# Four adaLN vectors from VectorE dot products to TensorE column groups, Fourier sums in two PSUM banks

## The chip, the cores and the metric

One core of a Trainium2 chip runs the whole layer as one program. The metric is the device time in microseconds of one execution. Three runs of the kernel before gave a median of 1030.87 us (1029.47 to 1032.01).

## The reference

One encoder layer on x of 1024 positions by 1024 channels, fp32, with a conditioning vector c of 1024:

```
cond = silu(c)
mod = cond @ w_ada + b_ada                      # 6144 values
sh1, sc1, gt1, sh2, sc2, gt2 = split(mod, 6)
h = rms_norm(x, g_pre_mix) * (1 + sc1) + sh1
u, v, rg_g, rg_x, ft_x = split(h @ w_in, ...)   # 1792 columns
y_gm = gelu(u) * spatial(layer_norm(gelu(v)))   # 256 channels
y_rg = two RG-LRU scans of conv(rg_x), gated by gelu(rg_g)   # 512
y_ft = Re(DFT2(ft_x)) @ w_f + b_f               # 256
x = x + gt1 * rms_norm(concat(rms_norm each) @ w_out, g_post_mix)
h = rms_norm(x, g_pre_ff) * (1 + sc2) + sh2
x = x + gt2 * rms_norm(square(relu(h @ w_ff1)) @ w_ff2, g_post_ff)
```

sh1 and sc1 are needed at once for the first normalised input. The other four vectors, gt1, sh2, sc2 and gt2, are needed only after the output projection has begun: these are the four late vectors of the change.

## The kernel before

Activations lie with channels on the 128 partitions and positions along the free dimension, as eight tiles of 1024 positions (`big`). Most products are made in three passes of fp32r on a high and a low part of each operand (`mm3`); ScalarE makes the high part of a weight tile and GpSimd or VectorE the low part (`split`, L170 and L171). All matmuls go through `mm` at L143, so the profile shows one line for them and the tiles tell them apart. A product of plain fp32 operands is one call of `mm` and two MATMUL rows in the trace.

The program is written as one long list of stages. First the input is normalised and the six columns of the input projection for the recurrence and the Fourier branch are made, the first half of the positions and then the second (`zk`). Then come the rest of the input projection (`z`, in full columns of two halves), the recurrence (`rg`, four tiles of two directions each, with matmuls `gz`), the Fourier branch (`ft_fold`, `ft_a`, `ft_b`, with matmuls `fa`, `fx` and `fe`), the spatial gating (`v_mm` with `vp`, `smix` with `rw` and `sp`), three group norms (`norm_group`, `norm_rg`, with matmuls `grs`), the output projection (`op`), the residual and second norm (`resid`) and the feed-forward block (`f`), which takes the last 600 us.

Beside that list run tasks, which are Python generators. A clock counts planned matmul time (`mm` adds columns/2400, four times that for fp32), and after each group of products `pump` runs the tasks that are due; each yields the planned time until its next step. `rg_all` is such a task, the norms are others, and so is `ada_all`, which is spawned right after the recurrence has been joined. This gives the order in which instructions are written; the framework then gives each engine its own order and sets the waits.

The adaLN vectors are dot products on VectorE: `ada(blk)` loads 128 rows of the transposed weight, 128 by 1024 (512 KB), and one instruction multiplies it with the condition, which lies spread over all partitions, and sums along the row into one column of `mod` (L454). There are 32 of them in `ada_all`, and 16 more of the first two vectors at the start of the program, which stay. `vec` adds the bias and, where needed, one and the gain. The loads use the tag `r`, four buffers of 512 KB, which the raw weight tiles of the input and output projections use as well; all of them are issued by SP.

PSUM has eight banks, all of one tag. In `ft_b` each of the two Fourier tiles takes four of them, one for each of the sums Ec, Es, Oc and Os: Es and Ec have 257 columns, Os and Oc 256. ScalarE copies Es and Os out (L648, L649), and four VectorE operations (L651 to L654) combine them with Ec and Oc.

Of the kernel before, what the change touches and what calls it, by code (L numbers as in the profile page):

```python
# [7 lines left out]
F32 = mybir.dt.float32  # L8
F32R = mybir.dt.float32r
AF = mybir.ActivationFunctionType  # L10
ALU = mybir.AluOpType
PSUM = bass.MemoryType.PSUM
MUL, ADD, SUB = ALU.mult, ALU.add, ALU.subtract
# [30 lines left out]
_n = 0  # L44
for _name, _w in (("b_ada", 48), ("g_pre_mix", 8), ("g_post_mix", 8), ("g_pre_ff", 8), ("g_post_ff", 8),
                  ("g_mix_out", 8), ("conv_w", 16), ("conv_b", 4), ("b_a", 8), ("b_x", 8), ("lam", 8),
                  ("ft_b", 2), ("ln_g", 2), ("ln_b", 2)):
    PV[_name] = (_n, _w)
    _n += _w
NPV = _n  # L50


@with_exitstack
def trunk(ctx, tc, xT, c, pv, ident, w_ada, w_k, w_in, w_v, gates, k1, k2, k3, gmft, w_out, w_ff1, w_ff2, out):
    nc = tc.nc
    const = ctx.enter_context(tc.tile_pool(name="const", bufs=1))
    pool = ctx.enter_context(tc.tile_pool(name="pool", bufs=21))
# [19 lines left out]
    def ctile(name, n, dt=F32, bufs=1):  # L77
        return const.tile([128, n], dt, name=name, tag=name, bufs=bufs)

    pvt = ctile("pvt", NPV)  # L80
    idt = ctile("idt", 128)
    ones = ctile("ones", 128)
    eps = ctile("eps", 1)
    mod = ctile("mod", 48)
    ab = ctile("ab", 56)
    sp = ctile("sp", 64)

    ctile("pad0", 8)
    HL = const.tile([128, 8, 2, 1024], F32R, name="HL", tag="HL")
    big = const.tile([128, 8, 1024], F32, name="big", tag="big")  # L90
    ctile("pad1", 8)
    a1, b1, a2, b2, g1, g2, bp1 = (ab[:, i * 8:i * 8 + 8] for i in range(7))

    def col(name, i, n=1):
        a = PV[name][0] + i
        return pvt[:, a:a + n]
# [3 lines left out]
    clock = [0.0]  # L100
# [17 lines left out]
    def spawn(gen, delay=0.0):  # L118
        return Task(gen, delay)
# [137 lines left out]
    cond = tt("cond")  # L257
    cps = pa("cb")
    sq0 = {}
    for h, (a, b) in enumerate(HALF):  # L260
        if h == 1:
            for k in (0, 1):
                sq0[k] = th("sq")
                A.activation(out=sq0[k], in_=big[:, k, 0:512], func=AF.Square)
        mm(cps[h], ones[0:1, :], crow[:, a:b], True, True)
        th0 = A.activation(out=cond[:, a:b], in_=cps[h], func=AF.Tanh, scale=0.5)
        V.scalar_tensor_tensor(out=cond[:, a:b], in0=cond[:, a:b], scalar=1.0, in1=cps[h], op0=ADD, op1=MUL)

    ssl, ssa = [None], [None]

# [89 lines left out]
    ps = [pb("zk%d" % i) for i in range(6)]  # L360
# [82 lines left out]
    ps = [pb("zk0"), pb("zk1")]  # L443
# [5 lines left out]
    evac_z(1, ps, 1, V)  # L449


    def ada(blk):
        r = load(w_ada[blk], tag="r")
        V.scalar_tensor_tensor(out=r, in0=r, scalar=0.5, in1=cond, op0=MUL, op1=MUL,  # L454
                               accum_out=mod[:, blk:blk + 1])

    def vec(dst, blk, gname, one):
        V.tensor_tensor(out=dst, in0=mod[:, blk:blk + 8], in1=col("b_ada", blk, 8), op=ADD)
        if one:
            V.tensor_scalar(out=dst, in0=dst, scalar1=1.0, scalar2=None, op0=ADD)  # L460
        if gname:
            V.tensor_tensor(out=dst, in0=dst, in1=col(gname, 0, 8), op=MUL)

    def ada_all():
        for blk in range(16, 48):
            ada(blk)
            yield ADY[0] if blk < ADY[1] else ADY[2]
        vec(g1, 16, "g_post_mix", False)
        vec(b2, 24, None, False)
        vec(a2, 32, "g_pre_ff", True)  # L470
        vec(g2, 40, "g_post_ff", False)


    xr_t, xs_t = {}, {}
# [110 lines left out]
    kt = {}  # L585
# [43 lines left out]

    def ft_b(t, at, ax):  # L630
        cosE = [kt[1][:, i * 257:i * 257 + 257] for i in range(3)]
        sinE = [kt[2][:, i * 257:i * 257 + 257] for i in range(2)]
        cosO = [kt[3][:, i * 256:i * 256 + 256] for i in range(2)]
        sinO = [kt[3][:, 512 + i * 256:768 + i * 256] for i in range(2)]
        ba = [at[:, j * 128:j * 128 + 128] for j in range(8)]
        ps = [pb("fe") for _ in range(4)]
        Ec, Es, Oc, Os = ps[0][:, 0:257], ps[1][:, 0:257], ps[2][:, 0:256], ps[3][:, 0:256]
        for dst, pairs in ((Es, ((ba[4], sinE[0]), (ba[5], sinE[1]))),
                           (Ec, ((ba[0], cosE[0]), (ba[1], cosE[1]), (ax, cosE[2]))),
                           (Os, ((ba[6], sinO[0]), (ba[7], sinO[1]))),  # L640
                           (Oc, ((ba[2], cosO[0]), (ba[3], cosO[1])))):
            for j, (w, x) in enumerate(pairs):
                mm(dst, w, x, j == 0, j == len(pairs) - 1)
            pump()
        y = big[:, 6 + t, :]
        b = col("ft_b", t)
        sn = [th("sn", F32, 257), th("sn", F32, 256)]
        A.copy(sn[0], Es)  # L648
        A.copy(sn[1], Os)  # L649
        Es, Os = sn  # L650
        V.scalar_tensor_tensor(out=y[:, 0:513:2], in0=Ec, scalar=b, in1=Es, op0=ADD, op1=SUB)  # L651
        V.scalar_tensor_tensor(out=y[:, 514:1024:2], in0=Ec[:, 255:0:-1], scalar=b, in1=Es[:, 255:0:-1], op0=ADD, op1=ADD)
        V.scalar_tensor_tensor(out=y[:, 1:512:2], in0=Oc, scalar=b, in1=Os, op0=ADD, op1=SUB)
        V.scalar_tensor_tensor(out=y[:, 513:1024:2], in0=Oc[:, ::-1], scalar=b, in1=Os[:, ::-1], op0=ADD, op1=ADD)  # L654

# [16 lines left out]
    for m in range(2, 6):  # L672
        p = {m: pb("zk")}
        for k in range(8):
            stage_mm(k, 1, p, (m,))
        evac_z(m, p, 1, V if m % 2 else A)
        if m == 2:
            kt[2] = load(k2, 770, "k2", "t")
            gm = load(gmft, 1024, "gm", "t")
        if m == 3:  # L680
            prep_to(1)
            for i, src, n in ((1, k1, 771), (3, k3, 1024)):
                kt[i] = load(src, n, "k%d" % i, "t")
# [23 lines left out]
            z_full(t, int(q[2]))  # L707
    kt.clear()
    join(trg)
    tad = spawn(ada_all(), 0.0)  # L710
    with tc.issue_after(rgl[0]):
        for t in range(2):
            A.activation(out=big[:, t, :], in_=big[:, t, :], func=AF.Gelu_apprx_tanh)
# [651 lines left out]
def _layout(inp):  # L1365
    import numpy as np

    f = lambda n: np.asarray(inp[n])
    cols = lambda v: v.reshape(-1, 128).T
    dt = f("x").dtype  # L1370
    pv = np.concatenate([
        cols(f("b_ada")[0]), cols(f("g_pre_mix")[0]), cols(f("g_post_mix")[0]), cols(f("g_pre_ff")[0]),
        cols(f("g_post_ff")[0]), cols(f("g_mix_out")[0]), cols(f("rg_conv_w")[0].reshape(-1)),
        cols(f("rg_conv_b")[0]), cols(f("rg_b_a")[0].reshape(-1)), cols(f("rg_b_x")[0].reshape(-1)),
        cols(f("rg_lam")[0].reshape(-1)), cols(f("ft_b")[0].reshape(-1)), cols(f("gm_ln_g")[0]),
        cols(f("gm_ln_b")[0])], axis=1)
    w_in = f("w_in")[0]
    wi = w_in.reshape(8, 128, 14, 128).transpose(2, 1, 0, 3).reshape(14, 128, 1024)[:8]
    wv = w_in[:, 256:512].reshape(2, 4, 128, 256).transpose(0, 2, 1, 3).reshape(2, 128, 1024)
    gates = np.zeros((4, 128, 2, 2, 128), dt)  # L1380
# [18 lines left out]
    k1 = np.concatenate([np.cos(tw * (2 * p * t % S)), np.cos(tw * (2 * p * (t + 128) % S)), c2], axis=1)  # L1399
    u = np.arange(64)  # L1400
    ang = 2 * np.pi * (u[:, None] * u[None, :] % 64) / 64
    ch = np.zeros((128, 2, 128))
    for e in range(2):
        ch[e * 64:e * 64 + 64, 0, e * 64:e * 64 + 64] = np.cos(ang) / 256
        ch[e * 64:e * 64 + 64, 1, e * 64:e * 64 + 64] = np.sin(ang) / 256
    k2 = np.concatenate([np.sin(tw * (2 * p * t % S)), np.sin(tw * (2 * p * (t + 128) % S)), ch.reshape(128, 256)], axis=1)
    k3 = np.concatenate([np.cos(tw * (o * t % S)), np.cos(tw * (o * (t + 128) % S)),
                         np.sin(tw * (o * (t + 1) % S)), np.sin(tw * (o * (t + 129) % S))], axis=1)
# [3 lines left out]
        "c": f("c")[0:1],  # L1412
        "pv": pv,
        "ident": np.eye(128, dtype=f32),
        "w_ada": f("w_ada")[0].T.reshape(48, 128, 1024),
        "w_k": w_in[:, 1024:].reshape(8, 128, 768),
        "w_in": wi,
        "w_v": wv,
# [32 lines left out]
```

## Time and profile before

| | before |
|---|---|
| median of 3 runs | 1030.87 us |
| profiled execution, its own time | 1031.33 us |
| its span, first to last instruction | 1029.5 us |
| mean granted TensorE clock | 0.970 |
| TensorE busy | 963.3 us, 94%, 4756 instructions |
| VectorE busy | 766.4 us, 74% |
| ScalarE busy | 501.0 us, 49% |
| GpSimd busy | 123.8 us, 12% |
| L454, the late dot products | 32, 48.5 us in all with what belongs to them |
| data moved | 191.59 MB, mean 186 GB/s |

The times of the rows are those of one profiled execution, counted from its first instruction. A group of instructions is written as line, engine, operation, output <- inputs, shapes and count. Idle time stands in brackets with the instruction that ended it. The granted clock of a stretch (PEclk) is a mean: 1.00 is 2.4 GHz, and 0.5 is 1.2 GHz.

### The profile page before, as it was taken

To read this page: it belongs to the slowest core of one execution; us is meant where nothing else is said; L and a number is where in the kernel's file an instruction comes from. 1 tells how busy PE (TensorE), PEld (TensorE's weight loads), DVE (VectorE), ACT (ScalarE), POOL (GpSimd) and SP (SyncE) were. 2 spreads that over 40 slices of the span, in tenths; PEclk is the share of its full clock that TensorE was granted. 3 is DMA by queue.
4 is the path that set the end of the run, shared out by engine and by line. 5 is a ranking of instruction groups with operands and counts; after the bars stand their busy time and mean duration, and the time that the engine had idled before them with its cause. 6 is when DMAs were issued, how large, how long until landed. Compare 5 with 4: busy or idle time off the path is not lost.

```text
span 1029.5 us, 13104 instructions
## 1 busy us (share of the span) xinstructions
PE 963.3 (94%) x4756; PEld 804.0 (78%) x4756; DVE 766.4 (74%) x1059; ACT 501.0 (49%) x764; POOL 123.8 (12%) x82
## 2 busy tenths in 40 slices
PE   6789975997899999999999999999999999999995
PEld 2568854896677997988888888888888888888995
DVE  6978888778897678897776776757665777688464
ACT  4454876622454355564544544545444455446311
POOL 4400391321140341000000000000000000000000
PEclk7989987998899999999999999999999999999998
DMA  9740200158235323054343343359899979987532
GB/s 343 286 142 21 82 24 18 62 202 288 102 131 177 129 97 113 32 183 185 132 179 138 133 191 126 123 198 331 297 392 341 362 269 335 328 277 258 187 133 93
DMA packets 80003, 191.59 MB, mean 186 GB/s; under 512 B 8769, under 2 KB 13121, under 8 KB 77890
## 3 DMA queue, kind: packets, MB, share of 16 engines
q1 hardware_dynamic: 76482, 186.56, 50.7%
q10 hardware_dynamic: 3456, 4.20, 1.1%
q8 instruction: 37, 0.61, 0.2%
q14 instruction: 28, 0.23, 0.1%
HBM read 144.58 MB, written 46.14 MB: 185 GB/s over the span
## 4 chain that ended last, share of the span: by engine, by line
PE 73%; DVE 14%; DMA 4%; ACT 4%; issue 3%; POOL 1%; SPq 0%; DVEq 0%; POOLq 0%
PE f L143 59%; PE op L143 6%; DMA raw<-in_w_ada_dram 3%; DVE raw L454 2%; PE z L143 2%; PE zk L143 2%; PE grs L143 1%; PE r L143 1%; DVE raw L291 1%; DVE HL L325 1%; DVE xr L481 1%; DVE big L537 1%; DMA big<-in_xT_dram 1%; ACT av L519 1%; DVE ss L279 1%
## 5 line engine op out<-in xcount | busy, mean ns | idle before, releaser
L143 PE MATMUL f<-x,x 128*128 128x512 f32 x768 | 236.2, 389 | 0.0
L143 PEld LDWEIGHTS f<-x,x 128*128 128x128 f32 x768 | 144.1, 188 | 29.8
L143 PE MATMUL f<-HL,wc 128*128 128x512 f32 x672 | 158.1, 390 | 0.0
L937 ACT CAST x<-R 128x1024 fp32r<-128x1024 f32 x96 | 100.3, 1053 | 110.8 <-DVE R L1131 56.0
L143 PE MATMUL f<-x 128*128 128x512 f32 x384 | 149.4, 389 | 0.0
L143 PEld LDWEIGHTS f<-HL,wc 128*128 128x128 f32 x672 | 125.0, 188 | 28.2 <-ACT big L1067 2.3
L948 DVE TENSOR_TENSOR x<-R,x 128x1024 fp32r<-128x1024 f32 x96 | 116.7, 1221 | 32.1 <-ACT x L937 30.7
L143 PE MATMUL f<-hc,wc 128*128 128x512 f32 x504 | 118.8, 389 | 0.0
L143 PEld LDWEIGHTS f<-hc,wc 128*128 128x128 f32 x504 | 94.6, 188 | 19.7
L143 PE MATMUL op<-HL,hi 128*128 128x256 f32 (+1 forms) x384 | 88.4, 324 | 0.0
L143 PEld LDWEIGHTS f<-x 128*128 128x128 f32 x384 | 72.1, 188 | 15.1
L143 PEld LDWEIGHTS op<-HL,hi 128*128 128x128 f32 x384 | 64.3, 190 | 6.5 <-issue 1.4
L1131 DVE TENSOR_TENSOR R<-R,o 128x512 f32<-128x512 f32 x64 | 43.6, 688 | 33.3 <-DMA o<-in_w_ff_dram 23.9
L143 PE MATMUL z<-HL,hi 128*128 128x512 f32 x192 | 63.3, 433 | 0.7 <-ACT ftg L614 0.7
L171 POOL TENSOR_TENSOR lo<-raw,hi 128x1024 fp32r<-128x1024 f32 x16 | 44.3, 2775 | 155.7 <-ACT hi L170 111.0
L143 PE MATMUL op<-HL,lo 128*128 128x256 f32 (+1 forms) x192 | 61.5, 320 | 0.0
L937 ACT CAST wc<-S 128x1024 fp32r<-128x1024 f32 x28 | 29.5, 1053 | 60.0 <-DVE S L1042 56.4
L454 DVE SCALAR_TENSOR_TENSOR raw<-raw,cond 128x1024 f32<-128x1024 f32 x32 | 48.5, 1521 | 13.4 <-DMA raw<-in_w_ada_dram 13.2
L948 DVE TENSOR_TENSOR wc<-S,wc 128x1024 fp32r<-128x1024 f32 x28 | 34.2, 1222 | 21.6 <-PE f L143 20.0
L143 PEld LDWEIGHTS z<-HL,hi 128*128 128x128 f32 x192 | 38.5, 204 | 11.9 <-issue 3.7
L143 PE MATMUL f<-HL,w 128*128 128x256 f32 x384 | 47.6, 285 | 0.0
L143 PEld LDWEIGHTS f<-HL,w 128*128 128x128 f32 x384 | 46.6, 192 | 0.6 <-issue 0.5
(298 smaller groups left out, 1637.8 us busy)
## 6 DMA issues: line engine op xcount, KB each, us to landing
raw<-in_w_ada_dram SPq DMA_DIRECT2D x48, 512.0 KB, 4.9
R<-Y SPq DMA_DIRECT2D x96, 256.0 KB, 4.8
R<-in_w_ff_dram SPq DMA_DIRECT2D x80, 256.0 KB, 5.0
raw<-in_w_ff_dram SPq DMA_DIRECT2D x32, 512.0 KB, 3.3
Y<-big SPq DMA_DIRECT2D x16, 1024.0 KB, 3.9
o<-in_w_ff_dram SPq DMA_DIRECT2D x64, 256.0 KB, 5.1
Y<-big SPq DMA_DIRECT2D x13, 768.0 KB, 3.4
SS<-R SPq DMA_DIRECT2D x32, 256.0 KB, 5.0
```

What stands on the lines that cost most here:

```text
L143: pe[0] = T.matmul(o, w, x, start=start, stop=stop, skip_group_check=more).ins
L171: (eng or V).tensor_tensor(out=lo, in0=src, in1=hi, op=SUB)
L279: ssl[0] = eng.tensor_tensor(out=ss, in0=ss, in1=sq, op=ADD).ins
L291: V.scalar_tensor_tensor(out=r1, in0=r1, scalar=0.5, in1=cond, op0=MUL, op1=MUL, accum_out=mod[:, 8 + k:9 + k])
L325: V.scalar_tensor_tensor(out=HL[:, k, 1, a:b], in0=xk, scalar=b1[:, k:k + 1], in1=HL[:, k, 0, a:b], op0=ADD, op1=SUB)
L454: V.scalar_tensor_tensor(out=r, in0=r, scalar=0.5, in1=cond, op0=MUL, op1=MUL, accum_out=mod[:, blk:blk + 1])
L481: V.scalar_tensor_tensor(out=xr[:, o0:o1], in0=z[:, i0:i1], scalar=col("conv_w", k * 4 + t), in1=xr[:, o0:o1], op0=MUL, op1=ADD)
L519: A.activation(out=av[:, a:b], in_=rr[h], func=AF.Exp, scale=m4[:, i:i + 1], bias=m4[:, i:i + 1])
L537: V.tensor_tensor_scan(ti, av, ti, 0.0, op0=MUL, op1=ADD)
L937: order[0] = A.copy(dst, src).ins
L948: V.tensor_tensor(out=lo, in0=raw, in1=hi, op=SUB)
L1131: V.tensor_tensor(out=w, in0=w, in1=self.o, op=ADD if q == "M5" else SUB)
```

## The change

`ada_all` now works on a weight laid out the other way round: eight chunks of 128 inputs by 1024 outputs for each vector. The condition is a column per chunk (`cc`, made from c, which now also comes in with the packed small vectors), and that column, spread to 32, is the stationary operand. The 1024 outputs of a chunk are taken as four groups of 256 columns; each group goes to its own 32 partitions of one PSUM bank (`ad`) and is summed over the eight chunks. Then ScalarE copies the bank, two small products with picked columns of the identity turn it into a 128 by 8 vector, and VectorE adds bias, one and gain as before. The task is spawned after the fifth of the six late input columns, with one step every 2.0 us of planned time; the clock books a step as one product of 256 columns, not four.

In `ft_b` Es and Ec share one bank, Os and Oc the other. Es loses its first and last column, which are zero, so that both fit into 512 columns; the two outputs that have no Es part come from a small ScalarE operation.

```diff
-ADY = (1.6, 32, 3)
+ADY = 2.0
...
+    cc = col("c", 0, 8)
+    ch = ctile("ch", 8)
+    A.activation(out=ch, in_=cc, func=AF.Tanh, scale=0.5)
+    V.tensor_scalar(out=ch, in0=ch, scalar1=0.5, scalar2=0.5, op0=MUL, op1=ADD)
+    V.tensor_tensor(out=cc, in0=cc, in1=ch, op=MUL)
...
     def ada_all():
-        for blk in range(16, 48):
-            ada(blk)
-            yield ADY[0] if blk < ADY[1] else ADY[2]
-        vec(g1, 16, "g_post_mix", False)
-        vec(b2, 24, None, False)
-        vec(a2, 32, "g_pre_ff", True)
-        vec(g2, 40, "g_post_ff", False)
+        for v, (dst, gname, one) in enumerate(((b2, None, False), (a2, "g_pre_ff", True),
+                                               (g1, "g_post_mix", False), (g2, "g_post_ff", False))):
+            i = (1, 2, 0, 3)[v]
+            p = pb("ad")
+            for k in range(8):
+                r = load(w_adn[i, k], tag="r")
+                for g in range(4):
+                    mm(p[g * 32:g * 32 + 32, 0:256], cc[:, k:k + 1].to_broadcast([128, 32]), r[:, g * 256:g * 256 + 256],
+                       k == 0, k == 7, True)
+                clock[0] -= 3 * 4 * 256 / 2400.0
+                yield ADY
+            sb = th("adr", F32, 256)
+            A.copy(sb, p[:, 0:256])
+            yield 1.0
+            q = p[:, 256:264]
+            for j in range(2):
+                mm(q[:, j:8:2], sb[:, j * 128:j * 128 + 128], idt[:, 0:128:32], True, True)
+            V.tensor_tensor(out=dst, in0=q, in1=col("b_ada", 16 + 8 * i, 8), op=ADD)
...
-        ps = [pb("fe") for _ in range(4)]
-        Ec, Es, Oc, Os = ps[0][:, 0:257], ps[1][:, 0:257], ps[2][:, 0:256], ps[3][:, 0:256]
+        ps = [pb("fe") for _ in range(2)]
+        Es, Ec, Os, Oc = ps[0][:, 0:255], ps[0][:, 255:512], ps[1][:, 0:256], ps[1][:, 256:512]
...
-        V.scalar_tensor_tensor(out=y[:, 0:513:2], in0=Ec, scalar=b, in1=Es, op0=ADD, op1=SUB)
+        A.activation(out=y[:, 0:513:512], in_=Ec[:, 0:257:256], func=AF.Identity, bias=b)
+        V.scalar_tensor_tensor(out=y[:, 2:512:2], in0=Ec[:, 1:256], scalar=b, in1=Es, op0=ADD, op1=SUB)
...
+        if m == 4:
+            tad = spawn(ada_all(), 0.0)
...
     join(trg)
-    tad = spawn(ada_all(), 0.0)
```

## Rows read from the trace of the kernel before

**Rows 1.** The page, first part: busy time, share and instructions of each engine.
```profile
PE 963.3 (94%) x4756; PEld 804.0 (78%) x4756; DVE 766.4 (74%) x1059; ACT 501.0 (49%) x764; POOL 123.8 (12%) x82
```

**Rows 2.** Windows: stretch, its length, each engine's busy time, PEclk, DMA share, GB/s.
```profile
114.00:166.00 52.00, 35.34 (x159) 28.28 (x157) 46.64 (x35) 36.79 (x59) 33.80 (x26) 0.87 0.16 58
166.00:177.40 11.40, 8.87 (x31) 6.97 (x31) 9.04 (x9) 11.15 (x18) 1.69 (x1) 0.80 0.00 1
177.40:247.40 70.00, 70.00 (x400) 61.85 (x398) 53.77 (x66) 28.69 (x39) 22.66 (x9) 0.98 0.45 156
247.40:275.00 27.60, 16.52 (x117) 12.26 (x115) 25.95 (x49) 11.86 (x19) 4.76 (x2) 0.88 0.48 179
275.00:311.00 36.00, 34.16 (x143) 26.87 (x144) 30.86 (x49) 18.48 (x29) 10.86 (x4) 0.91 0.40 139
311.00:1029.00 718.00, 705.22 (x3571) 600.05 (x3569) 505.79 (x702) 334.31 (x502) 24.84 (x25) 1.00 0.57 205
```

**Rows 3.** Waits of TensorE, 100 to 410 us: total, times, longest.
```profile
PE fe L143 <- ACT at L75: 9.6, 1, 9.6
PE grs L143 <- DVE dg L219: 8.2, 2, 6.7
PE grs L143 <- DVE gss L552: 4.4, 1, 4.4
...
PE gz L143 <- DVE big L535: 2.5, 1, 2.5
PE fe L143 <- DVE big L654: 2.1, 1, 2.1
...
PE grs L143 <- DVE gss L805: 0.3, 1, 0.3
```

**Rows 4.** The chain that ended last, around 253 us: start, length, what.
```profile
252.10 1.23 DVE raw L454 x2
...
253.65 0.61 DVE dg L219
```

**Rows 5.** Instructions on the tile `raw`, the late dot products: ns min/median/max, first, last start.
```profile
L454 DVE SCALAR_TENSOR_TENSOR raw<-raw,cond x32: 1183/1224/3410, 199.6 to 323.5; 128x1024 f32<-128x1024 f32 x32
```

**Rows 6.** Timeline of TensorE, 254 to 275 us: start, length, what.
```profile
254.40 2.05 PE L143 MATMUL grs<-dg,ones 128*128 128x512 f32 x2 [6.66 <-DVE dg L219]
...
258.31 0.40 PE L143 MATMUL z<-HL,lo 128*128 128x512 f32 x1
258.63 0.66 PE L143 MATMUL rw<-gm,ones 128*64 128x128 f32 x8
...
260.42 3.50 PE L143 MATMUL sp<-gm,vs 128*64 128x128 f32 x60
263.85 0.73 PE L143 MATMUL z<-HL,hi 128*128 128x512 f32 x2
264.42 0.39 PE L143 MATMUL z<-HL,lo 128*128 128x512 f32 x1
...
269.63 0.61 PE L143 MATMUL z<-HL,hi 128*128 128x512 f32 x2
270.09 0.39 PE L143 MATMUL z<-HL,lo 128*128 128x512 f32 x1
274.89 1.54 PE L143 MATMUL grs<-ones,gss 128*128 128x1 f32 x8 [4.42 <-DVE gss L552]
```

**Rows 7.** Timeline of TensorE, 151 to 170 us, the Fourier matmuls.
```profile
151.70 1.06 PE L143 MATMUL fa<-ftg,fo 128*128 128x128 f32 x8
...
152.82 1.90 PE L143 MATMUL fe<-k,at 128*128 128x257 f32 x8
...
154.99 1.89 PE L143 MATMUL fe<-k,at 128*128 128x256 f32 x8
166.44 3.48 PE L143 MATMUL fe<-k,at 128*128 128x257 f32 x8 [9.56 <-ACT at L75]
```

**Rows 8.** Timeline of VectorE, around 270 us: a late dot product.
```profile
270.27 1.21 DVE L454 SCALAR_TENSOR_TENSOR raw<-raw,cond 128x1024 f32<-128x1024 f32 x1
```

More of the change, by code (lines that the diff above doesn't have):

```diff
@@ L46 @@
                   ("g_mix_out", 8), ("conv_w", 16), ("conv_b", 4), ("b_a", 8), ("b_x", 8), ("lam", 8),
-                  ("ft_b", 2), ("ln_g", 2), ("ln_b", 2)):
+                  ("ft_b", 2), ("ln_g", 2), ("ln_b", 2), ("c", 8)):
     PV[_name] = (_n, _w)
@@ L53, in trunk @@
 @with_exitstack
-def trunk(ctx, tc, xT, c, pv, ident, w_ada, w_k, w_in, w_v, gates, k1, k2, k3, gmft, w_out, w_ff1, w_ff2, out):
+def trunk(ctx, tc, xT, c, pv, ident, w_ada, w_adn, w_k, w_in, w_v, gates, k1, k2, k3, gmft, w_out, w_ff1, w_ff2, out):
     nc = tc.nc
@@ L86, in trunk @@
     sp = ctile("sp", 64)
-    ctile("pad0", 8)
     HL = const.tile([128, 8, 2, 1024], F32R, name="HL", tag="HL")
     big = const.tile([128, 8, 1024], F32, name="big", tag="big")
-    ctile("pad1", 8)
+    ctile("pad", 16)
     a1, b1, a2, b2, g1, g2, bp1 = (ab[:, i * 8:i * 8 + 8] for i in range(7))
@@ L449, in trunk @@
     evac_z(1, ps, 1, V)
[L452 to L462, printed above, removed]
-    def ada_all():
-        for blk in range(16, 48):
-            ada(blk)
-            yield ADY[0] if blk < ADY[1] else ADY[2]
-        vec(g1, 16, "g_post_mix", False)
-        vec(b2, 24, None, False)
-        vec(a2, 32, "g_pre_ff", True)
-        vec(g2, 40, "g_post_ff", False)
+    def ada_all():
+        for v, (dst, gname, one) in enumerate(((b2, None, False), (a2, "g_pre_ff", True),
[16 more added lines that the diff above has]
+            V.tensor_tensor(out=dst, in0=q, in1=col("b_ada", 16 + 8 * i, 8), op=ADD)
+            if one:
+                V.tensor_scalar(out=dst, in0=dst, scalar1=1.0, scalar2=None, op0=ADD)
+            if gname:
+                V.tensor_tensor(out=dst, in0=dst, in1=col(gname, 0, 8), op=MUL)
     xr_t, xs_t = {}, {}
@@ L631, in ft_b @@
         cosE = [kt[1][:, i * 257:i * 257 + 257] for i in range(3)]
-        sinE = [kt[2][:, i * 257:i * 257 + 257] for i in range(2)]
+        sinE = [kt[2][:, i * 257 + 1:i * 257 + 256] for i in range(2)]
         cosO = [kt[3][:, i * 256:i * 256 + 256] for i in range(2)]
@@ L646, in ft_b @@
         b = col("ft_b", t)
-        sn = [th("sn", F32, 257), th("sn", F32, 256)]
+        sn = [th("sn", F32, 255), th("sn", F32, 256)]
         A.copy(sn[0], Es)
@@ L650, in ft_b @@
         Es, Os = sn
-        V.scalar_tensor_tensor(out=y[:, 0:513:2], in0=Ec, scalar=b, in1=Es, op0=ADD, op1=SUB)
-        V.scalar_tensor_tensor(out=y[:, 514:1024:2], in0=Ec[:, 255:0:-1], scalar=b, in1=Es[:, 255:0:-1], op0=ADD, op1=ADD)
+        A.activation(out=y[:, 0:513:512], in_=Ec[:, 0:257:256], func=AF.Identity, bias=b)
+        V.scalar_tensor_tensor(out=y[:, 2:512:2], in0=Ec[:, 1:256], scalar=b, in1=Es, op0=ADD, op1=SUB)
+        V.scalar_tensor_tensor(out=y[:, 514:1024:2], in0=Ec[:, 255:0:-1], scalar=b, in1=Es[:, ::-1], op0=ADD, op1=ADD)
         V.scalar_tensor_tensor(out=y[:, 1:512:2], in0=Oc, scalar=b, in1=Os, op0=ADD, op1=SUB)
@@ L1375, in _layout @@
         cols(f("rg_lam")[0].reshape(-1)), cols(f("ft_b")[0].reshape(-1)), cols(f("gm_ln_g")[0]),
-        cols(f("gm_ln_b")[0])], axis=1)
+        cols(f("gm_ln_b")[0]), cols(f("c")[0])], axis=1)
     w_in = f("w_in")[0]
@@ L1414, in _layout @@
         "ident": np.eye(128, dtype=f32),
-        "w_ada": f("w_ada")[0].T.reshape(48, 128, 1024),
+        "w_ada": f("w_ada")[0][:, 0:2048].T.reshape(16, 128, 1024),
+        "w_adn": f("w_ada")[0][:, 2048:].reshape(8, 128, 4, 1024).transpose(2, 0, 1, 3),
         "w_k": w_in[:, 1024:].reshape(8, 128, 768),
```

## The prediction

> **What bounds the kernel now.** First the page: TensorE is busy 94% of the span, VectorE 74%, ScalarE 49% [rows 1]. A change therefore shows in the time only where TensorE stands still, runs at a lower granted clock, or gets more or less to do. So I next cut the span where the change lies and looked at how much TensorE is missing in each stretch [rows 2]. From 177.4 to 247.4 us it is busy 70.00 of 70.00 us, and after 311 us it is dense again but for 12.8 us in 718, which the change does not touch. The missing time is in three places: 16.7 us in 114 to 166, 2.5 us in 166 to 177.4, and 11.1 + 1.8 us in 247.4 to 311. Third, the waits of TensorE name who ended these holes [rows 3]: before 177 us the recurrence's and the Fourier branch's hand-offs (ScalarE `at` 9.6 us, VectorE L535 2.5, L654 2.1), after 247 us the norm's `dg` (8.2 us, of which one is 6.7) and `gss` (4.4 and 0.3). The longest of the late ones, 6.66 us, is the present price of the adaLN vectors: `dg` comes at 253.65 behind two dot products of L454 that had waited for their weights [rows 4, 6]. The chain of waits runs through those loads and dots for some 58 us before, but beside a full TensorE, where they cost nothing.
>
> **What goes.** 32 dot products of 1.224 us leave VectorE, 39 us in all [rows 5]. Worth on the path: the 6.66 us hole goes, since `dg` needs only a short chain that starts with sums made at 241 us. With it goes the slow restart: from 254.40 to 258.63 TensorE does two `grs` matmuls of 512 columns and six `z`, in 4.23 us; at the pitches seen elsewhere (0.216 per 256 columns of fp32, so 0.43; 0.23 for a `z`) it is 2.24 us, so 2.0 are clock [rows 6, 7]; the granted clock of that stretch is 0.88 [rows 2]. The hole of 4.42 us before 274.89 stays in the main: it starts from matmuls `sp` and runs through VectorE work that remains; one dot of 1.2 us in it, at 270.27, goes [rows 8]. The other `dg` wait (8.2 - 6.7 = 1.5) and the `gss` L805 wait (0.3) have dots ahead of them and go. In 275 to 311 the clock is 0.91, which is 0.09 x 36 = 3.2 us; half of it, 1.6, I count as given back because the hole ahead of it is only shortened. Sum of what comes back: 6.7 + 2.0 + 1.2 + 1.5 + 0.3 + 1.6 = 13.3 us. Bounds: 6.7 (the one hole alone) and 6.7 + 2.0 + 4.4 + 1.5 + 0.3 + 3.2 = 18.1 (every hole and all the clock).
>
> **What TensorE gets.** 32 steps (four vectors x eight chunks) of four fp32 products, 32 columns stationary, 256 moving, each to its own 32 partitions of PSUM. An fp32 product is two MATMUL rows (the two `grs` above are one call), so a step is eight instructions. One with 256 columns takes (1.89 - 0.38)/7 = 0.216 us when they follow one another [rows 7]. No row shows four column groups. The nearest row has two: `sp`, 64-column products alternating between two halves of the array, 60 in 3.50 us, that is (3.50 - 0.27)/59 = 0.055 each, against (1.06 - 0.28)/7 = 0.112 for the same 128 columns on the whole array [rows 6, 7]. Two halves do overlap by a full factor of two. Bounds of a step: 8 x 0.216 / 4 = 0.43 with four abreast, 0.86 if only pairs overlap, 1.73 if none does. I take 0.43: the factor with two was complete. To that comes the change between whole array and groups. Going in, `z` at 258.31 to `rw` at 258.63 is 0.32 instead of 0.23; going out, the last `sp` at 263.65 to `z` at 263.85 is 0.20 instead of 0.11, and `z` to `z` (two, 0.57 instead of 0.46, as at 269.63 to 270.09) loses 0.11 more [rows 6]. Together 0.29 per visit, with a floor of 0 if the next step follows at once. A step: 0.72 us; 32 make 23 us. Each vector ends with four instructions of 4 columns for the turn into columns, about 0.11 each, 0.45. The planner books 0.43 a step, so its clock runs ahead of the engine.
>
> The Trainium skill (TensorE: Matmul & The Clock Gate, Packing small matmuls) reports three column groups giving 2.38 times, less than three. Carried to four it would be some 3.2 times, an estimate from that page: 0.55 for the products of a step instead of 0.43, and 2 us more on the path over 18 steps. The full factor in the two-group row speaks against it, and no row here has more than two.
>
> **Where the steps fall.** The task now starts after the fifth of the six late input columns, about 114 us, not after the recurrence. Steps are due every 2.0 us of planned matmul time and are looked at only between groups of 0.64 or 1.28, so about 2.4. At the planner's own prices (0.213 for 512 columns, four times that in fp32) the matmuls between 114 and 166.4 come to some 29 us, those from 166.4 to 177.4 to 6.5, those from 177.4 to 247.4 to 63. So about 12 steps run before 166.4, two between, and the other 18 after 177.4; the last is planned some 20 us before 247.4.
> - The 12 before 166.4: 8.7 us plus one turn, beside 16.7 us of holes. Cost nothing. If the holes were not there, or if a step came ahead of a matmul that the recurrence waits for, up to 9.2.
> - 166.4 to 177.4: two steps, +1.4. The wait for L654 is for PSUM banks of the first Fourier tile; with two banks per tile instead of four I count its 2.1 us as gone. The first eight Fourier matmuls take 3.48 us after a 9.56 us hole, and 1.90 when TensorE was running [rows 7]; with steps in the hole, 1.6 comes back. Against that, +1.3 for what is put into the hand-offs: the sums of Es now wait in one bank behind six matmuls of Ec (6 x 0.216 = 1.3), one more bank is held by the vector for eight steps, and VectorE and ScalarE wait for the turn. Net -1.0, bounds -3.7 and +6.
> - After 177.4: TensorE is full there, so 18 x 0.72 = 13.0 and three turns 1.3: +14.3. If ready steps are drawn forward into the earlier holes, down to 8.
> The loads (32 of 512 KB) only move earlier, into stretches with a DMA share of 0.16 and 0.00 [rows 2], and share four buffers with the weights to be split. SP's queue is where a late step would hold a weight load behind it; these weights are used 20 us after their load is due, so nothing. The condition as a column (one tanh and two operations on 8 columns at the start) lies beside the input loads: nothing. The small ScalarE operation on two Fourier columns, twice: inside the 1.3.
>
> **Sum.** -1.0 + 14.3 - 13.3 = 0.0 against the profiled execution's own 1031.33 us, which lies 0.46 above the median shown. Forecast 1030.9 us: no change. About 0.3%, 3 us, is what a measurement of this kernel can tell from none.
>
> **Rivals.**
> - Only pairs of column groups overlap (slower). Place: the 20 steps after 166.4. Price: 0.86 - 0.43 = 0.43 each, +8.6: 1039.5. It decides as soon as a step takes more than 0.9 us. For it: no row has four; against: the pair is perfect. With no overlap at all, 20 x 1.3 = +26: 1057.
> - The freed banks let ready work fill the 9.6 us hole (faster). The next input products have their operands before 166 us and stand behind the Fourier sums; if banks, not the order written out, kept them there, 8 us of the 10 come forward: 1023. For it: the L654 wait shows a shortage of banks. Against: the 9.6 us hole ended with `at`, which the change does not hasten.
> - The held bank or the buffers lengthen the recurrence (slower): L535 already keeps `gz` 2.5 us for a bank [rows 3]; with one fewer, the next release of that chain and the turn's wait on VectorE make +5: 1036.
> - The late holes stay although the dots are gone, because the same VectorE work is waited for: only 6.7 of 13.3 comes back, +6.6: 1037.5.
>
> **From this to the numbers.** Forecast 0.40 (own range 1026 to 1036); pairs 0.14, no overlap 0.04; filled hole 0.25; bank 0.10; holes stay 0.07. Range 1020 to 1042: it leaves out no overlap, the far ends of pairs and filled hole, under 0.2. Faster by over 0.3%: 0.24 of the filled hole and 0.12 of the forecast's lower end, 0.36. Slower: all of pairs and no overlap, most of the next two and 0.05 of the forecast, 0.36. Within: 0.28.
>
> **What would show it.** The `ad` matmuls: eight in a step with starts that give 0.43 us, not 0.86 or 1.7, and about 0.3 us lost around them. The wait for `dg` of 6.7 us gone. The stretch from the first full input column to the last `z` before the first `grs` some 14 us longer, the stretch to 311 some 13 us shorter. The `fe` wait for L654 gone, the one for `at` still there. The prediction is wrong if the hole before 166 closes, if a step costs over 0.9 us, or if holes appear in the full stretch.

## The result and the profile after

The changed kernel takes 1059.67 us (median of four runs, 1058.04 to 1061.14) against 1030.61 for the kernel before on the same chip: a ratio of 1.0281, 95% interval 1.026 to 1.0302. The forecast was 1030.9, range 1020 to 1042: wrong by 28.8 us, and outside its range. The profiled execution has a span of 1057.2 us, 27.7 more than before.

First part of the page after, beside [rows 1]:

```profile
PE 995.5 (94%) x5028; PEld 809.5 (77%) x5028; DVE 725.6 (69%) x997; ACT 505.3 (48%) x773; POOL 126.2 (12%) x82
```

VectorE lost 41 us of work, TensorE is busy 32 us more. Where the time came in, from the first starts of tiles (us from the span's start):

| landmark | before | after | later by | this stretch alone | forecast of it |
|---|---|---|---|---|---|
| first full column of `z` | 177.4 | 184.1 | 6.7 | +6.7 | -1.0 |
| last `z` ahead of the norm's first `dg` matmul | 247.4 | 264.7 | 17.3 | +10.6 | +14.3 |
| first `op` | 288.1 | 310.4 | 22.3 | +5.0 | -13.3 |
| first `f` | 389.4 | 414.1 | 24.7 | +2.4 | 0 |
| end | 1029.5 | 1057.2 | 27.7 | +3.0 | 0 |

Windows of the changed kernel with these bounds, columns as in [rows 2]:

```profile
114.00:166.00 52.00, 42.36 (x237) 28.02 (x236) 44.01 (x33) 31.35 (x49) 32.24 (x26) 0.87 0.50 175
166.00:184.10 18.10, 15.93 (x95) 12.52 (x94) 14.69 (x13) 18.04 (x32) 3.28 (x1) 1.00 0.31 117
184.10:264.60 80.50, 80.48 (x527) 61.82 (x526) 29.77 (x55) 31.43 (x47) 22.45 (x8) 1.00 0.42 151
264.60:311.00 46.40, 30.53 (x170) 23.73 (x170) 35.79 (x44) 27.00 (x39) 17.09 (x6) 0.81 0.23 80
```

The dense stretch stayed dense (80.48 of 80.50 us). The stretch that was to get shorter has 15.9 us without TensorE work. Waits of TensorE, 100 to 410 us, beside [rows 3]:

```profile
PE grs L143 <- DVE gss L564: 15.9, 2, 9.3
PE gp L143 <- DVE big L388: 4.8, 1, 4.8
PE ad L143 <- DMA raw<-in_w_adn_dram: 4.8, 3, 2.7
PE fe L143 <- ACT at L75: 1.6, 1, 1.6
```

The waits for `dg` are gone as forecast, and so is all but 1.6 us of the one of 9.6 us for `at`, which was to stay. In their place stand two long waits for `gss` and, early, new ones of `gp` and `ad`.

The price of a step came out as forecast. The tile `ad`, and TensorE's timeline around a step in the dense stretch:

```profile
L143 PE MATMUL ad<-raw,pvt x256: 379/379/636, 114.2 to 238.2; 128*32 128x256 f32 x128
```

```profile
186.90 0.63 PE L143 MATMUL z<-HL,lo 128*128 128x512 f32 x2
187.46 0.64 PE L143 MATMUL ad<-raw,pvt 128*32 128x256 f32 x8
188.02 1.20 PE L143 MATMUL z<-HL,hi 128*128 128x512 f32 x4
189.06 0.63 PE L143 MATMUL z<-HL,lo 128*128 128x512 f32 x2
```

Four steps that stood ready together, in the hole ahead of `at`:

```profile
166.55 1.93 PE L143 MATMUL ad<-raw,pvt 128*32 128x256 f32 x30
```

Thirty instructions of 0.379 us each are done in 1.93, so eight take (1.93 - 0.38)/29 x 8 = 0.43 us: the four groups run fully side by side. Among `z`, from the `z` group at 186.90 to the next at 188.02 is 1.12 us instead of some 0.46, and that next group of four takes 1.04 instead of 0.93. A step costs 0.66 + 0.11 = 0.77 us (forecast 0.72), and the others of the dense stretch cost the same.

The long wait for `gss` is made on VectorE. GpSimd's and VectorE's timelines of the changed kernel:

```profile
250.38 4.76 POOL L171 TENSOR_TENSOR lo<-raw,hi 128x1024 fp32r<-128x1024 f32 x2 [15.27 <-ACT hi L170]
273.13 14.73 POOL L171 TENSOR_TENSOR lo<-raw,hi 128x1024 fp32r<-128x1024 f32 x5 [18.00 <-ACT hi L170]
```

```profile
273.91 1.40 DVE L570 SCALAR_TENSOR_TENSOR big<-big,pvt,grs 128x512 f32<-128x512 f32 x2
275.22 0.74 DVE L786 SCALAR_TENSOR_TENSOR sg<-sp,pvt,tg 128x512 f32<-128x512 f32 x1
275.88 0.93 DVE L820 TENSOR_TENSOR gss<-gss,gsq 128x512 f32<-128x512 f32 x1
276.74 3.43 DVE L808 TENSOR_TENSOR big<-big,sg 128x1024 f32<-128x1024 f32 x1
280.08 2.83 DVE L820 TENSOR_TENSOR gss<-gss,gsq 128x512 f32<-128x512 f32 x1
282.84 2.82 DVE L171 TENSOR_TENSOR HL<-big,HL 128x512 fp32r<-128x512 f32 x1
285.59 2.82 DVE L820 TENSOR_TENSOR gss<-gss,gsq 128x512 f32<-128x512 f32 x1
288.33 0.68 DVE L564 TENSOR_TENSOR gss<-gss,gsq 128x512 f32<-128x512 f32 x1
```

GpSimd makes five low parts of output-projection weights in one block. Beside it, VectorE operations of 128 by 512 with two SBUF operands take 2.8 us (the first of them, at 275.88, only 0.93) instead of the 0.68 that the last row shows just after the block; those with one operand in PSUM (`sg` from `sp`, L570 from `grs`) keep their 0.70 to 0.74. The Trainium skill (SBUF — State Buffer, Who interferes with whom) states that a VectorE instruction with two SBUF inputs contends with a GpSimd instruction that reads SBUF, and that one with at most one SBUF input outside the two-port modes does not. The rows agree in both halves.

In the kernel before the low parts stand apart, but one of them falls beside the VectorE operation for which TensorE waits in the 4.42 us hole of [rows 6]. Two of its GpSimd rows, and that operation:

```profile
271.93 2.36 POOL L171 TENSOR_TENSOR lo<-raw,hi 128x1024 fp32r<-128x1024 f32 x1 [4.40 <-ACT hi L170]
283.74 4.71 POOL L171 TENSOR_TENSOR lo<-raw,hi 128x1024 fp32r<-128x1024 f32 x2 [9.45 <-ACT hi L170]
```

```profile
272.01 2.82 DVE L552 TENSOR_TENSOR gss<-gss,gsq 128x512 f32<-128x512 f32 x1
```

So the price of a low part beside this chain, 2.1 us, stood in the trace that the prediction was made from.

### The profile page after: what moved, and what is told of

Read it like the earlier page. It is cut to its first block, busy times and chain, and to the rows that moved or that the text cites. A ratio compares the mean times of both kernels' runs of the same rounds, so it can differ in the third digit from the quotient of the medians.

```text
span 1057.2 us, 13585 instructions
## 1 busy us (share of the span) xinstructions
PE 995.5 (94%) x5028; PEld 809.5 (77%) x5028; DVE 725.6 (69%) x997; ACT 505.3 (48%) x773; POOL 126.2 (12%) x82
## 4 chain that ended last, share of the span: by engine, by line
PE 83%; DVE 7%; POOL 3%; ACT 2%; issue 2%; DMA 2%; SPq 0%; DVEq 0%; POOLq 0%; ACTq 0%
PE f L143 57%; PE op L143 7%; PE z L143 6%; PE zk L143 5%; PE vp L143 2%; PE ad L143 1%; PE grs L143 1%; PE gz L143 1%; PE r L143 1%; DMA xh<-in_xT_dram 1%; DVE gss L820 1%; DMA big<-in_xT_dram 1%; DVE HL L332 1%; DVE xh L1267 0%; PE rx L143 0%
## 5 line engine op out<-in xcount | busy, mean ns | idle before, releaser
L143 PE MATMUL f<-HL,wc 128*128 128x512 f32 x672 | 161.7, 395 | 0.0
L952 ACT CAST x<-R 128x1024 fp32r<-128x1024 f32 x96 | 100.2, 1053 | 110.5 <-DVE R L1146 56.3
L143 PE MATMUL op<-HL,hi 128*128 128x256 f32 (+1 forms) x384 | 91.2, 332 | 0.0
L143 PE MATMUL zk<-HL,wkb 128*128 128x512 f32 x192 | 48.7, 401 | 0.0
```

What stands on the lines that cost most here:

```text
L952: order[0] = A.copy(dst, src).ins
```

## The experiments

**Which half of the change.** The Fourier sums alone; the vectors alone; the vectors begun where the old task began.

```diff
# e1: before, with ft_b of the change
# e2: changed, with ft_b of before
# e3: changed, and:
-        if m == 4:
-            tad = spawn(ada_all(), 0.0)
     join(trg)
+    tad = spawn(ada_all(), 0.0)
```

> The kernel before with the Fourier part of the change alone (two PSUM banks, the small ScalarE operation). Theory H (hand-offs): the two banks are no cause of the 29 us; 1029 to 1032, the wait of fe for L654 (2.1 us) gone and nothing else moved by more than 2 us. Rival F (the shared banks delay the recurrence): the first full input column starts some 6 us later than 177.4 us, as in the changed kernel (184.1), and the time is about 1037.

> The changed kernel with the Fourier sums back in four banks. Theory H: the late vectors alone make the loss, 1058 to 1064. Rival F: with the four banks back, 6 us or more come back, 1053 or less. A third way: four banks and the held bank together starve PSUM, and it is slower than 1064.

> The changed kernel, but the vectors' task starts where it did before, after the recurrence has been joined. The loads then share the four buffers with the output projection's weights again. Theory W (the loss after 264 us comes from the output projection's weights: their loads no longer alternate with the vectors' loads, so five GpSimd splits run in one block, 273 to 288 us, beside VectorE operations that take 2.8 us instead of 0.7): no such block, the first full input column again near 177 us, all 32 steps on the path (32 x 0.77 + 2 = 27) less the 6.7 us hole: about 1045 to 1052. Rival O (the holes come from the order in which VectorE got its work without the dot products): the holes of 9.3 and 6.5 us stay, 1058 or more.

Each ratio is to the kernel before on the same chip. Measured: e1 1029.54 (ratio 0.9993, 0.9979 to 1.0007), e2 1062.26 (1.0304, 1.0277 to 1.0331), e3 1047.27 (1.0165, 1.0143 to 1.0187). The Fourier half is neutral, as counted, and the wait for L654 is gone. The vectors, with the constants and padding that came with them, make the whole loss. Begun late, they leave the recurrence alone and GpSimd's low parts stand apart; the two long holes are not there, and the loss is 1.65% instead of 2.81%.

**The late stage.** The vectors left out altogether; then the low parts moved; then only the dots left out.

```diff
# e4: before, and (late vectors' sums are zero):
-            ada(blk)
+            if blk == 16:
+                V.memset(mod[:, 16:48], 0.0)
# e5: e4, and; e8: changed, and:
-        wlist.append((("out", k), w_out[k], G))
+        wlist.append((("out", k), w_out[k], V))
# e6: before, with a one-column operation in place of each late dot
```

> The kernel before with the 32 late loads and dot products left out, their sums taken as zero: that part of the result is left out. It shows by itself what their absence gives back. The prediction's term: 13.3 us come back, 1017. Theory W: the 6.7 us hole goes, but the output projection's weights come in one block and open holes of some 10 to 15 us around 270 to 290: 1030 to 1040. Rival O expects the same holes, but with VectorE operations of normal length (0.7 us) in them.

> As e4 (late loads and dot products left out, their sums zero), and the low parts of the eight output projection weights made on VectorE instead of GpSimd. Theory W (GpSimd's block of splits stretches the VectorE operations on the way to the third norm from 0.7 to 2.8 us): no stretched operation, the hole of 9.4 us before 268 shrinks to 5 or less although VectorE gets 8 x 1.2 us more to do, 1026 to 1031. Rival O (order alone): the hole stays at 8 to 10 us, 1034 or more.

> The kernel before with the 32 late loads kept in the four shared buffers, but each dot product replaced by one operation on a single column, so the late vectors are not computed. Theory W: as long as these loads alternate with the output projection's weights, the GpSimd splits stay apart, the holes of 9.4 and 6.5 us of e4 do not come, and VectorE's relief shows: 1018 to 1027, with a hole before dg left where VectorE still waits for a load. Rival O (VectorE's order without the long operations makes the holes): 1033 or more, as e4.

> The changed kernel with the low parts of the eight output projection weights on VectorE instead of GpSimd. Theory W: the hole of 9.3 us before 289 shrinks to 5 or less, 1052 to 1056. Rival O: hole and time stay, 1058 to 1062.

Measured: e4 1034.02 (1.0037, 1.0021 to 1.0052), e5 1021.81 (0.9903, 0.9879 to 0.9927), e6 1038.08 (1.0058, 1.0038 to 1.0078), e8 1047.47 (1.0147, 1.0119 to 1.0175).

e4 refutes the term that failed, by itself: without dots, loads or steps the kernel is not 13.3 us faster than before but 0.37% slower. GpSimd's block and TensorE's waits in e4:

```profile
252.11 14.71 POOL L171 TENSOR_TENSOR lo<-raw,hi 128x1024 fp32r<-128x1024 f32 x5 [17.91 <-ACT hi L170]
```

```profile
PE grs L143 <- DVE gss L553: 16.0, 2, 9.4
```

With the eight low parts on VectorE, which gets more work by that, e4 gets 12.2 us shorter (e5) and the changed kernel 12.2 as well (e8) by the medians, 13.8 by the ratios; both are faster than theory W had them. VectorE's operations of the norm in e5, then TensorE's waits in e5 and in e8:

```profile
258.19 0.68 DVE L806 TENSOR_TENSOR gss<-gss,gsq 128x512 f32<-128x512 f32 x1
258.78 1.22 DVE L794 TENSOR_TENSOR big<-big,sg 128x1024 f32<-128x1024 f32 x1
259.92 0.68 DVE L806 TENSOR_TENSOR gss<-gss,gsq 128x512 f32<-128x512 f32 x1
260.52 0.69 DVE L171 TENSOR_TENSOR HL<-big,HL 128x512 fp32r<-128x512 f32 x1
261.12 0.68 DVE L806 TENSOR_TENSOR gss<-gss,gsq 128x512 f32<-128x512 f32 x1
```

```profile
PE grs L143 <- DVE gss L553: 6.2, 2, 5.7
```

```profile
PE grs L143 <- DVE gss L564: 6.3, 2, 5.8
```

So GpSimd's low parts beside the norm cost 12 us. With them out of the way one sees what the absence of the dots is worth. The stretch from the last `vp` to the first `op`, in the kernel before and in e5, columns as in [rows 2]:

```profile
237.00:288.10 51.10, 40.02 (x220) 31.53 (x218) 41.88 (x80) 22.06 (x34) 11.51 (x5) 0.87 0.48 172
```

```profile
236.60:280.70 44.10, 37.89 (x219) 29.93 (x218) 35.06 (x63) 26.66 (x40) 0.00 (x0) 0.94 0.18 60
```

TensorE stands idle 6.2 us instead of 11.1: the `dg` hole is gone (6.7) and the `gss` hole of 4.4 has shrunk to 0.5, but one of 5.7 has opened ahead of the last `gss` sum before `op`, where the kernel before does not wait:

```profile
287.25 0.95 PE L143 MATMUL grs<-ones,gss 128*128 128x1 f32 x8
```

The same matmuls take 37.9 us instead of 40.0, at a granted clock of 0.94 instead of 0.87. In all e5 gains 7.0 us in this stretch.

What keeps the low parts apart in the kernel before is not the sharing of the buffers with the late loads, as theory W had it: e6 keeps all 32 loads and has a block all the same (and a hole of 7.3 us).

```profile
259.42 11.96 POOL L171 TENSOR_TENSOR lo<-raw,hi 128x1024 fp32r<-128x1024 f32 x4 [22.40 <-ACT hi L170]
```

What is left is the dots' time on VectorE, which holds the norm's operations and the buffers longer. That is argued by elimination and not shown, and through which of the two it works was not separated.

**Other orders and the low parts elsewhere.**

```diff
# e7: e1, and:
+    tgf = [spawn(norm_group((6, 7), 256), 1.0)]
     v_mm(0)
     v_mm(1)
...
-    tgf = [spawn(norm_group((6, 7), 256), 1.0)]
# e9: before, and; e12: e3, and:
-        wlist.append((("out", k), w_out[k], G))
+        wlist.append((("out", k), w_out[k], V))
```

> The kernel before with the Fourier part of the change, and the Fourier group's norm task started ahead of the two v products instead of behind the layer norm; nothing left out. If the 6.7 us hole before dg is only a matter of where this norm stands, it closes and the restart's 2 us with it: 1021 to 1024. Rival: VectorE's wait for a weight load stands ahead of dg there too and holds TensorE inside the v products: 1028 or more.

> The kernel before with one edit: the low parts of the eight output-projection weight tiles are made by VectorE, not GpSimd; the dot products stay on VectorE. Theory W (the GpSimd low parts cost only where several of them follow one another beside the norm's VectorE work): in the kernel before they stand apart, so little is won, and VectorE gets 8 x 1.2 = 10 us more beside 39 us of dots: 1028 to 1032 us. Rival 1 (each GpSimd low part costs wherever it stands): some 12 us come back as with the vectors left out, 1019. Rival 2 (VectorE, with dots and low parts, becomes late for the norm): holes of TensorE before the norm sums grow, 1035 or more.

> The changed kernel with the vectors begun only after the recurrence (as in the earlier run at 1047 us), and the eight output-projection low parts on VectorE. Theory W (GpSimd low parts cost where they form a block beside the norm): there the GpSimd low parts already stood apart, so 1043 to 1048 us. Rival (each of them costs wherever it stands): 12 us come back, 1035.

Measured: e7 1038.64 (1.0061, 1.0038 to 1.0083): the `dg` hole, 5.4 us, only moved ahead into the `vp` matmuls, and two of 5.7 for `gss` came behind it. e9 1034.53 (1.0025, 1.0007 to 1.0042): between theory W and the second rival; the holes for `dg` and `gss` shrink to 5.0 and 2.1, but `op` now waits 4.1 us for low parts from VectorE. e12 1042.92 (1.0116, 1.0091 to 1.0142): 4.4 us better than e3, a little more than W allowed and far from the rival's 12. The low parts cost 12 us as a block; where they stand apart, moving them won 4.4 us (e3 to e12) or nothing (before to e9).

**The early loss.** Without the late loads; with a bank for each step.

```diff
# e10: changed, and:
-                r = load(w_adn[i, k], tag="r")
-                    mm(..., r[:, g * 256:g * 256 + 256],
+                    mm(..., pvt[:, 0:1].to_broadcast([128, 256]),
# e11: changed, and:
-            p = pb("ad")
             for k in range(8):
+                p = pb("ad")
...
-                       k == 0, k == 7, True)
+                       True, True, True)
```

> The changed kernel without the 32 late weight loads: the column-group products take a resident column, repeated, as moving operand (so the four vectors are not the layer's). Products, banks and turns stay. Open is the early loss: first full input column 6.7 us later than before. Theory S (the steps wait for loads that wait for shared buffers, and hold TensorE behind them): the two waits of 1.8 and 2.7 us near 155 and 158 us go and with them what hangs on them; first full column at 179 us or earlier, total about 1053. Theory H (the PSUM bank held through eight steps takes it from the gated products): the 4.8 us wait for a bank near 135 us stays, first full column at 183 to 185, total 1058 to 1061. Theory T (the steps themselves lie on the path there, no hole takes them): also 183 to 185 us, but without the 4.8 us wait.

> The changed kernel with a new PSUM bank for each step, given back after it, and no summing over the eight chunks (so the four vectors hold the last chunk only). Loads, products and turns stay. Theory H (held bank): the 4.8 us wait near 135 us goes, first full input column at 178 to 180 us, total about 1054. Theory S (shared load buffers): the waits near 155 and 158 us stay, first full column at 182 to 185 us, total 1057 to 1061.

TensorE's timeline: the changed kernel, then e11. The matmuls `gp` make `ftg`, which every `fa` reads; `at` is ScalarE's copy of `fa`.

```profile
134.85 2.08 PE L143 MATMUL gp<-gm,k 128*128 128x128 f32 x8 [4.82 <-DVE big L388]
...
155.03 0.64 PE L143 MATMUL ad<-raw,pvt 128*32 128x256 f32 x8 [1.81 <-DMA raw<-in_w_adn_dram]
...
158.35 1.07 PE L143 MATMUL ad<-raw,pvt 128*32 128x256 f32 x4 [2.68 <-DMA raw<-in_w_adn_dram]
...
170.04 2.00 PE L143 MATMUL fe<-k,at 128*128 128x255 f32 x8 [1.56 <-ACT at L75]
```

```profile
135.09 1.08 PE L143 MATMUL ad<-raw,pvt 128*32 128x256 f32 x8 [3.37 <-DVE big L388]
...
166.60 2.07 PE L143 MATMUL fe<-k,at 128*128 128x255 f32 x4 [10.08 <-ACT at L75]
168.60 1.08 PE L143 MATMUL ad<-raw,pvt 128*32 128x256 f32 x8
```

The same place in e10, and a row of ScalarE in the changed kernel:

```profile
168.01 3.78 PE L143 MATMUL fe<-k,at 128*128 128x255 f32 x8 [3.23 <-ACT at L75]
```

```profile
163.83 0.27 ACT L639 COPY ax<-fx 128x128 f32<-128x128 f32 x1 [7.46 <-PE fx L143]
```

Measured: e10 1056.44 (1.0244, 1.0218 to 1.027), first full column at 183.2 us, `at` at 168.0 instead of 170.0, the 4.8 us wait still there. So the loads make 2.0 of the 3.6 us by which `at` is late, but only 1 us of the early loss, and some 2 behind it. ScalarE's row shows how: the steps' waits for loads at 155 and 158 us stand ahead of `fa` and `fx` in TensorE's order, and ScalarE's copy of `fx`, which stands ahead of the recurrence's next operations and of `at` in its own, waits 7.46 us. e11 1061.34 (1.0296, 1.0272 to 1.0321): `gp` no longer waits (a step waits there instead, 3.37 us for the same operation), no step waits for a load at 155 or 158 us, and `at` comes at 166.6 as before [rows 7], not 170.0. So the held bank and the loads together make `at` 3.4 us late; e11 takes both waits away, and the bank's own share was not separated. But e11 gains nothing: six steps now stand between `at` and the first full column, which comes at 186.6. H was right that `at` would come back and wrong on the time.

**The placement.** The last 5.4 us of the table lie where no step runs. The long weight stretch of the feed-forward block, in the kernel before and after:

```profile
L143 PE MATMUL f<-HL,wc x672: 387/389/435, 438.3 to 705.7; 128*128 128x512 f32 x168
```

```profile
L143 PE MATMUL f<-HL,wc x672: 388/394/418, 462.4 to 734.1; 128*128 128x512 f32 x168
```

The same matmuls take 271.7 us instead of 267.4. The mean difference of the start times of neighbours with `HL` as moving operand is 233.3 ns for 512 columns against 227.3, already in the `zk` of the first 114 us, and so in every later stretch. Products on the same weight tiles whose moving operand is a working tile (`f<-hc,wc`) keep 226.7 and 227.7 ns, so it is not the place of the weight tiles alone. The change also moves tiles: in front of the working tiles it adds 8 columns to the packed vectors, 8 for `ch` and 8 of padding, and takes away 8 in front of `HL`. `HL` stays where it was, and the working tiles lie 16 columns, 64 bytes, further from it.

```diff
-    ctile("pad0", 8)
...
-    ctile("pad1", 8)
+    ctile("pad", 16)
# e13: changed, without the line ctile("pad", 16): tiles lie as before
# e14: before, ctile("pad1", 24): 64 bytes higher; e16: ctile("pad1", 16): 32 bytes
# e15: e12, without ctile("pad", 16)
```

> The changed kernel with only the 16 columns of padding ahead of the working tiles taken out; every tile after them lies 64 bytes lower, as in the kernel before. Found in the traces: products of 512 columns with HL follow one another every 233.3 ns in the changed kernel from the first input columns on (40 to 114 us, long before a vector step), 226.7 ns in the kernel before and in every run with its placement. Theory P (the place of the weight tiles against HL sets the pitch): 226.7 ns again, and some 8 to 10 us come back (292 zk, 288 z, 672 in the feed-forward block and about 250 in the output projection, 6.5 ns each): 1050 us. Rival (the pitch hangs on something else in the changed program): 233.3 ns and 1057 to 1061.

> The kernel before with 16 more columns of padding, so that the working tiles lie where the changed kernel has them (64 bytes higher); nothing else. Theory P: 233.3 ns pitch and 8 to 10 us slower, 1039 to 1041. Rival: 226.7 ns and 1029 to 1032.

> The kernel before with 8 more columns of padding: working tiles 32 bytes higher, half of the shift of the change. Theory P says the pitch hangs on the distance to HL but not how: bounds 226.7 ns (1029 to 1032) and 233.3 ns (1039 to 1041); if 32 bytes give a third value, the place counts in steps smaller than 64 bytes. Rival: no change in pitch and time.

> The changed kernel without that padding, with the vectors begun after the recurrence and the output-projection low parts on VectorE (with padding: 1042.9). Theory P: 1033 to 1035, that is the 32 steps cost about what the placement and the GpSimd block did not. Rival: 1041 to 1045.

Measured: e13 1056.69 (1.025, 1.0224 to 1.0276), e14 1036.29 (1.0061, 1.0045 to 1.0078), e16 1036.36 (1.0061, 1.0046 to 1.0076), e15 1038.07 (1.0079, 1.0062 to 1.0095). The stretch in e13 (one line was taken out, so L142) and in e14:

```profile
L142 PE MATMUL f<-HL,wc x672: 387/390/436, 464.6 to 731.9; 128*128 128x512 f32 x168
```

```profile
L143 PE MATMUL f<-HL,wc x672: 388/395/419, 441.0 to 712.6; 128*128 128x512 f32 x168
```

267.3 and 271.6 us: the pitch follows the padding in both directions, and 32 bytes do the same as 64. Theory P holds for the pitch (only the working tiles were moved, never `HL`); its price was put too high (8 to 10). Exchanged both ways it is worth, by the ratios, 6 us in the kernel before and 3 in the changed one, 4 from e12 to e15. Products of 256 columns go the other way, 120 to 117 ns. From the first `op` to the end e13 takes 742.6 us, the changed kernel 746.8 and the kernel before 741.4, so 4.2 of the 5.4 us are the placement; the other 1.2 were not followed.

**The dots moved instead of replaced.**

```diff
# e17: e1, and; e18: e17 with the eight low parts on VectorE:
-            yield ADY[0] if blk < ADY[1] else ADY[2]
+            yield 22.0 if blk == 26 else 1.6 if blk < 26 else 2.0
```

> The kernel before with the Fourier sums in two banks, and the 32 dot products kept on VectorE, but with a pause of 22 us of planned time after the eleventh and a quicker pace after it (2.0, not 3), so that most of the dots that stand ahead of the first norm's dg move behind it. Theory D (the dots ahead of dg make its hole of 6 us): it falls to 3 us or less, 1024 to 1028. Theory W (with the dots away from there the output-projection weights arrive together and GpSimd makes their low parts in a block beside the norm): that hole falls too, but holes of 7 to 9 us come behind it, 1030 to 1036.

> The same with the eight output-projection low parts on VectorE. Theory W: no GpSimd block, so what is left is the hole before gss of 5 us and the smaller dg hole: 1022 to 1028, faster than both kernels. Rival (VectorE with 10 us of low parts and the dots after the pause is late for the output projection, as it was with the dots at their old pace): 1031 to 1036.

Measured: e17 1040.18 (1.0084, 1.0062 to 1.0106), e18 1028.88 (0.9983, 0.9969 to 0.9997). GpSimd in e17, TensorE's waits in e17, then in e18:

```profile
260.12 11.26 POOL L171 TENSOR_TENSOR lo<-raw,hi 128x1024 fp32r<-128x1024 f32 x4 [25.37 <-PE sp L143]
```

```profile
PE grs L143 <- DVE gss L552: 14.3, 2, 7.4
...
PE grs L143 <- ACT gsq L551: 4.0, 1, 4.0
```

```profile
PE grs L143 <- DVE gss L552: 7.8, 3, 5.9
PE grs L143 <- DVE dg L219: 3.1, 1, 3.1
```

W again, though at a price above its range: with the dots away from the norm (none starts between 251.2 and 273.1 us, where the kernel before has those at 259.3 and 270.3) the block of low parts comes, and with it two holes for `gss`; without the block 11.3 us come back. e18 computes the whole layer. It is far ahead of the changed kernel, but only 1.7 us below the one before by the ratio (1.1 by the medians), with an interval that just leaves out no change.

## Why the prediction was wrong

- **What goes (13.3 us to come back): this step failed.** From the last `vp` to the first `op` the kernel before takes 51.1 us (237.0 to 288.1), the changed one 56.3 (254.1 to 310.4), e4 56.0 and e5 44.1 (236.6 to 280.7). So with the low parts out of the way the dots do give back 7.0 us. That this is near the lower bound of the step, "the one hole alone" (6.7), is chance: the `dg` hole went (6.7), the `gss` hole lost 3.9 and not 1.2, the clock gave 2.1, and the new hole of 5.7 took most of it away. The small waits (1.5 and 0.3) lie behind the first `op` and gave nothing: from there to the first `f` the kernel before and e5 both take 101.3 us. In the changed kernel not even the clock came back (0.81 in 264.6 to 311 us, below the 0.88 and 0.91 of [rows 2]), and the block of low parts takes another 12. The prediction wrote that `dg` "needs only a short chain" and that the second hole "runs through VectorE work that remains"; it priced that work at the durations it had, and never asked what else would move when VectorE had time. GpSimd's row in [rows 2] for 247.4 to 275 us (2 low parts, 4.76 us) shows the block that was not there yet, and the 2.82 us operation at 272.01 us shows what it would cost. The fourth rival, late holes that stay, had the right place at a chance of 0.07, and a price of 6.6 instead of 18. The rival "no overlap", 1057 us, came near the measured time by luck: the overlap was complete.
- **The first stretch: -1.0 forecast, +6.7 measured.** 3.6 of it are the third rival, the held bank or the buffers: `at` comes at 170.0 us instead of 166.4. The other 3.1 lie between `at` and the first full column (14.1 us instead of 10.9). The sums `fe` of the first Fourier tile, which the kernel before makes ahead of the hole (3.9 us, from 152.82 in [rows 7]), now come behind it, and 12 products `gz` come ahead of the column instead of behind it (2.7 us, which is only order); against that the wait for L654 (2.1) and the slow restart (1.5) are gone, as forecast. A sign of being wrong that the prediction named, the hole before 166 us closing, did come. As products the 12 steps before 166 us cost nothing (10 of them in e11, with `at` on time).
- **The dense stretch: +14.3 forecast, +10.6 measured.** With the 2.7 us of `gz` that moved out, 13.3: right in size, for 16 steps (12.3 us) and three turns instead of 18 and three; four ran in the hole ahead of `at`, where two were forecast. Full overlap of four groups was right, and so was the price of changing between groups and the whole array. The Trainium skill's figure for three groups (TensorE: Matmul & The Clock Gate, Packing small matmuls) would have given 0.55 us for a step's products, as an estimate; the row of thirty `ad` instructions gives 0.43, and the measurement decides. What all steps cost together is seen between e5 and e8, neither of which has the block: 25.7 us, of which 3 to 6 are placement.
- **After 311 us: 0 forecast, +5.4 measured.** Not a term of the sum at all: 4.2 of it are the placement. The change's padding and constants move tiles, and the prediction gave that no term.
- **The Fourier banks: right.** e1 is within 0.1% of before, the wait for L654 gone. The second rival (filled hole, 0.25) fell: in e1, with the banks free, the wait for `at` is still 9.9 us.

The terms that missed: 18.3 (late stage) + 7.7 (first stretch) + 5.4 (after 311 us) - 3.7 (dense) = 27.7 us, the growth of the span. Of the 18.3, 12 are shown by e5 and e8; the other 6 are the difference between 13.3 and the 7.0 of e5, for the most part the hole of 5.7.

Left open: why the dots keep the low parts apart (buffers or VectorE's order), how the early loss is shared between bank and loads, and the hole of 5.7 to 6.5 us ahead of the last `gss` sum, which the kernel before does not have and e4, e5, e8 and e18 do.

## What to carry to other kernels

Work that is taken off an engine gives back what its wait was worth only if nothing else moves into the place: before a hole is booked as gain, look at which engine becomes ready earlier then, and whether it shares anything with the chain that follows the hole. Here GpSimd, 12% busy, made VectorE four times slower on the chain, and one operation of 2.82 us among others of 0.68 was the sign of it beforehand. And a change of constants or padding is a change of addresses: compare the pitch of the untouched matmuls first.

## What the runs showed of the hardware

- VectorE operations of 128 by 512 on two SBUF operands take 2.82 us beside GpSimd's subtraction of 128 by 1024, 0.68 without it; operations with one operand in PSUM keep 0.70 to 0.74.
- Four 32-column groups of fp32 products with 256 moving columns run side by side; a visit among whole-array matmuls costs 0.77 us, of which some 0.3 is the change there and back.
- The pitch of 512-column products with `HL` is 227.3 ns in the kernel before and 233.3 with 32 or 64 bytes more between `HL` and the weight tiles.
